# Pool makes the low parts of the projections' weights, the indexer sees 384 query tokens, and the branch for crowded experts goes behind the stores

## The chip, the cores and the metric

The kernel runs on one core of one Trainium2 chip (trn2). The metric is the device time of one execution in microseconds (us). The engines are TensorE (PE; PEld is its loading of weights), VectorE (DVE), ScalarE (ACT), GpSimd (POOL) and SyncE (SP); SP issues nearly all transfers between the chip's main memory and the on-chip memory, which 16 transfer engines carry out.

## What is computed

One decoder layer over 512 tokens of width 1024, then a final norm. In float32, shortened from the reference:

```
h = rms_norm(x, g_mix)
qa, ka, va, qb, kb, vb, qi, ki, wi, ga, gb = split(h @ w_in)     # 8 heads of 64 each; qi: 8 indexer heads; ki: one
qa, ka, qb, kb, qi, ki = rope(...)
o_a = block-sparse attention(qa, ka, va)                         # at 512 tokens: plain causal attention
score[t, s] = sum_h wi[t, h] * relu(qi[t, h] . ki[s])            # indexer, s <= t
o_b = attention(qb, kb, vb) over the 128 best keys s of each t by score
x = x + (sigmoid(ga) * (o_a @ w_proj_a) + sigmoid(gb) * (o_b @ w_proj_b)) @ w_out
h2 = rms_norm(x, g_ffn)
group = argmax of 4 group logits; two best of the 8 experts in that group, with gates
x = x + sum over the two experts e of gate * ((silu(h2 @ w1[e]) * (h2 @ w3[e])) @ w2[e])     # 32 experts
return rms_norm(x, g_final)
```

A query t < 128 has at most 128 admissible keys, so all of them are selected for it whatever the scores are.

## The kernel before

**Precision.** A product that has to be nearly float32 is made of three products of a one-pass format: a value is split into a high part (ACT copies it to that format) and a low part (the value minus the high part, a subtraction by DVE or Pool). `split` is this pair; `halves_of` loads a chunk of weights in two halves of 512 KB, splits the first with DVE's subtraction and the second with Pool's. A chunk is 1024 x 256 weights of one projection; `chunk(name)` loads one of the 20 that pass through it (two more come through `load_split` and `halves_of` at the start), at raised priority. Three buffers hold raw halves ("raw"), two pairs hold high and low parts ("wh", "wl").

**Front half.** PE's program is an order written out by hand (`in_order`); the other engines are ordered by a planner that places instructions by dependence and priority. `proj_T` makes one block of 128 columns of a chunk, transposed, for all 512 tokens: 8 steps over the contraction of three products each. `two_blocks` makes both blocks of a chunk, `rope_of` rotates one, `q_stack` and `k_stack` split the result for the attention (`k_stack` has four subtractions on Pool for each block). `attend` runs one quad of heads in 8 steps, and between scores, transposes and values it lets a share of other work run (`run(work, cost)`; a step of `proj_T` counts 0.64). That other work is `others`: the indexer's queries qi0, then qi1, qa1 and ka1 mixed with `idx_scores` (the indexer's scores for the token blocks 1 to 3; block 0 is not scored), values, queries and keys of branch b, gates and merging. `topk` on DVE finds 128 keys for each query.

**Experts.** 32 experts in 8 groups of 4, weights in 24 pieces of 1 MB for each group (8 for w1, 8 for w3, 4 + 4 for the two halves of w2). `fetch` requests the next piece into a free slot of 8 KB per partition, `spend` frees a slot and fetches again; SP's program is in order (`ordered`). Each expert has room for 32 tokens (CAP). Per group: `up` with w1, `silu_of`, `gated`, `up` with w3, `hidden`, gathering of the next group's tokens, `hidden_T`, `down` for each half of the width, `parts_of` (split of the result), `combine` (products that spread the results to the tokens, and DVE's addition to x).

If an expert has more than 32 tokens, `rest_of_tokens` does the rest in a loop. That branch stands before group 6 (lines 1018 to 1032): the order by hand is closed, every engine loads the largest count (`nc.values_load`) and compares it. With these inputs no expert has more than 32 tokens, so the loop is skipped. Ahead of the branch 8 pieces are requested from ACT's queue (`BRIDGE`), and a few slots are held back for it (`kept`).

**End.** For the last group the second half of w2 is mixed with combining the first half (`first_half`); then for each block of 128 tokens: combine the second half, sum of squares, power on Pool, scaling of the first half on ACT and of the second on DVE, and two stores (8 stores of 256 KB in all). This end is ordered by the planner.

Of the kernel before, what the change touches and what calls it, by code (L numbers as in the profile page):

```python
# [21 lines left out]
P = 128  # L22
# [18 lines left out]

REST = 6
BRIDGE = 8
# [96 lines left out]
def layer_kernel(ctx: ExitStack, tc: tile.TileContext, xT, x, w_ki, w_ch, w_ab, w_out, g_mix, g_ffnk, g_fin, w_r, b_r,  # L140
# [46 lines left out]
    def load_split(src, pair=None, place=None):  # L187
        hi, lo = pair or w_pair()
        for _ in halves_of(hi, lo, src, place):
            pass  # L190
# [121 lines left out]
    def q_stack(name, ps):  # L312

        qs = Q[name[1:]] = S.get([P, 4, T], F32R, name)
        for b in range(2):
            r = rope_of(ps[b])
# [289 lines left out]
    gfn, have, kept = [], {}, [0]  # L606

    def fetch(n, queue=sp):
        for _ in range(n):
            if not todo or len(S.idle) <= kept[0]:  # L610
# [8 lines left out]
            queue.dma_start(out=have[q, i], in_=w_e[q, i])  # L619
# [261 lines left out]
    def transposed(gsel):  # L881
# [4 lines left out]
        selT = t2([P, T], F32R, name="selT", tag="selT")  # L886
# [5 lines left out]
    def gated(sel, G):  # L892
# [4 lines left out]
        return transposed(gsel.rearrange("p t e s -> p t (e s)"))  # L897
# [21 lines left out]
    def parts_of(ys):  # L919

        out = []
        for h in range(2):
            y = t2([P, 2, 512], F32R, name="y", tag="y")
# [4 lines left out]
    def combine(selT, y, c, t):  # L928
# [6 lines left out]
        dve.tensor_tensor(o, ps, o, ALU.add)  # L935

# [79 lines left out]
    waiting = []  # L1016
    for q in range(NQ):
        if q == REST:
            for f in waiting:
                f()  # L1020
            waiting = []
            kept[0] = 0
            fetch(BRIDGE, act)
            bridge.close()
            in_order.close()
            ordered.close()
            rv = nc.values_load(cint[0:1, 0:1], min_val=0, max_val=T)
            with tc.If(rv > CAP):
                rest_of_tokens()
            ordered.enter_context(tc.manual_schedule(engines={mybir.EngineType.SP}))  # L1030
            in_order.enter_context(tc.manual_schedule(engines={mybir.EngineType.PE}))
            fetch(len(S.idle))
        if q == REST - 1:
            bridge = ExitStack()
            bridge.enter_context(tc.manual_schedule(engines={mybir.EngineType.Activation}))
# [9 lines left out]
        selT, gate = gated(sel, G[:, :, QE * q:QE * (q + 1)])  # L1045
        h3 = two(pt_, "tr", "h3")
        for k in range(NK):
            if q == REST - 1 and k == 2:

                kept[0] = len(S.idle) + BRIDGE + 6  # L1050
# [113 lines left out]
```

## Time and profile before

| | before |
|---|---|
| median of 3 runs | 937.04 us (935.4 to 939.02) |
| the profiled execution's own time | 939.58 us |
| its span, first to last instruction | 937.5 us |
| PE busy | 875.8 us, 93% |
| DVE busy | 426.5 us, 45% |
| ACT busy | 278.5 us, 30% |
| POOL busy | 178.6 us, 19% |
| granted TensorE clock, mean | 0.984 |

Busy is time in which an engine had an instruction under way; products on PE overlap, so a busy PE is not PE at its peak. Queue names end in q (SPq); a row of SPq is a request for a transfer or a wait of that queue, not the transfer. In rows of operations, "out<-in" gives the program's names, then partitions x elements and type; a bracket at the end gives the idle time before and what ended it.

### The profile page before, as it was taken

The page shows a single profiled execution, that of the slowest core. Times are in us where ns is not written, and L with a number is a line of the kernel's source. Part 1 is how long each engine was busy: PE and PEld are TensorE (multiplying, and loading weights), DVE is VectorE, ACT ScalarE, POOL GpSimd, SP SyncE. Part 2 cuts the span into 40 slices and gives each one's busy share as a digit, 9 for nine tenths or more (in the row PEclk, how much of TensorE's full clock was granted, in tenths as well). Part 3 has the DMA queues.
Part 4 walks back from the last instruction along what each step waited for, and adds up shares of the span by engine and source line. Part 5 has one row for each costly group of instructions (what it writes and reads, how often), then busy time and mean ns, then how long its engine had stood idle before and what let it go on. Part 6 is the DMA issues. An engine that isn't in the chain of part 4 may idle for free. (4 is left out here: it accounts for less than half of the span.)

```text
span 937.5 us, 15635 instructions
## 1 busy us (share of the span) xinstructions
PE 875.8 (93%) x6436; PEld 518.0 (55%) x6436; DVE 426.5 (45%) x981; ACT 278.5 (30%) x585; POOL 178.6 (19%) x115
## 2 busy tenths in 40 slices
PE   7999989989999999899999999999998989599885
PEld 5897769768777877689834343422423223133221
DVE  3747899998545554641722323231421302313114
ACT  4546654553443554533510100010100100001013
POOL 1494335243114820600300000000000000000003
PEclk9999999999999999899999999999999999799998
DMA  8422112112214221574589999999999999989995
GB/s 324 153 81 68 46 46 91 45 45 91 68 68 180 90 91 50 188 289 180 208 359 420 420 420 421 420 419 420 419 421 420 421 420 419 417 330 418 422 419 201
DMA packets 41261, 244.49 MB, mean 261 GB/s; under 512 B 4961, under 2 KB 5345, under 8 KB 16609
## 3 DMA queue, kind: packets, MB, share of 16 engines
q1 hardware_dynamic: 40032, 235.06, 63.4%
q10 hardware_dynamic: 1152, 8.39, 2.2%
q8 instruction: 51, 0.84, 0.4%
q14 instruction: 26, 0.20, 0.1%
HBM read 241.33 MB, written 2.10 MB: 260 GB/s over the span
## 5 line engine op out<-in xcount | busy, mean ns | idle before, releaser
L868 PE MATMUL h<-we,xs 128*32 128x512 f32 x2048 | 237.4, 600 | 25.9 <-DMA we<-in_w_e_dram 16.7
L868 PEld LDWEIGHTS h<-we,xs 128*32 128x32 f32 x2048 | 59.0, 110 | 179.3 <-issue 111.9
L875 PE MATMUL y<-we,hT 128*32 128x512 f32 x1024 | 116.1, 595 | 3.0 <-DMA we<-in_w_e_dram 3.0
L266 PE MATMUL mm<-xh,wh 128*128 128x512 f32 x272 | 110.2, 405 | 0.8 <-DVE bias L404 0.8
L268 PE MATMUL mm<-xh,wl 128*128 128x512 f32 x272 | 107.7, 396 | 0.0
L267 PE MATMUL mm<-xl,wh 128*128 128x512 f32 x272 | 107.7, 396 | 0.0
L173 POOL TENSOR_TENSOR wl<-raw,wh 128x1024 fp32r<-128x1024 f32 (+1 forms) x23 | 64.4, 2801 | 135.0 <-ACT wh L172 76.9
L1094 POOL TENSOR_TENSOR fo<-x,gfn 128x512 f32<-128x512 f32 x4 | 5.0, 1272 | 446.4 <-DVE x L935 446.4
L935 DVE TENSOR_TENSOR x<-cps,x 128x512 f32<-128x512 f32 x64 | 43.3, 688 | 82.0 <-PE cps L933 81.9
L875 PEld LDWEIGHTS y<-we,hT 128*32 128x32 f32 x1024 | 30.1, 109 | 74.5 <-issue 56.7
L909 DVE SCALAR_TENSOR_TENSOR silu<-silu,gate,h 128x512 f32<-128x512 f32 x16 | 12.0, 748 | 114.7 <-PE h L868 113.7
L268 PEld LDWEIGHTS mm<-xh,wl 128*128 128x128 f32 x272 | 51.2, 188 | 12.4
L266 PEld LDWEIGHTS mm<-xh,wh 128*128 128x128 f32 x272 | 51.4, 189 | 11.8 <-issue 1.2
L267 PEld LDWEIGHTS mm<-xl,wh 128*128 128x128 f32 x272 | 51.3, 189 | 9.6
L172 ACT CAST wh<-raw 128x1024 fp32r<-128x1024 f32 (+1 forms) x46 | 45.6, 1028 | 32.2 <-DMA raw<-in_w_ch_dram 13.2
L903 ACT ACTIVATE silu<-h 128x512 f32<-128x512 f32 x16 | 9.6, 598 | 146.7 <-PE h L868 119.2
L172 ACT CAST y<-y 128x512 fp32r<-128x512 f32 x32 | 18.7, 586 | 113.6 <-PE y L875 113.6
L916 ACT COPY hT<-htr 128x512 f32<-128x512 f32 x16 | 8.7, 588 | 147.3 <-PE htr L914 147.3
L173 DVE TENSOR_TENSOR y<-y,y 128x512 fp32r<-128x512 f32 x32 | 22.0, 688 | 54.3 <-ACT y L172 54.3
L448 ACT ACTIVATE ps<-e,st 128x128 f32<-128x128 f32 (+3 forms) x64 | 33.5, 524 | 43.7 <-DVE st L447 43.5
L173 DVE TENSOR_TENSOR wl<-raw,wh 128x1024 fp32r<-128x1024 f32 (+1 forms) x23 | 31.9, 1386 | 27.2 <-ACT wh L172 22.6
L687 PE MATMUL mm<-woh,mt 128*128 128x256 f32 x128 | 36.5, 285 | 1.2 <-DVE mt L655 1.2
(201 smaller groups left out, 1569.2 us busy)
## 6 DMA issues: line engine op xcount, KB each, us to landing
we<-in_w_e_dram SPq DMA_DIRECT2D x184, 1024.0 KB, 19.8
raw<-in_w_ch_dram SPq DMA_DIRECT2D x44, 512.0 KB, 4.1
we<-in_w_e_dram ACTq DMA_DIRECT2D x8, 1024.0 KB, 16.1
raw<-in_w_ab_dram SPq DMA_DIRECT2D x8, 512.0 KB, 3.9
wraw<-in_w_out_dram SPq DMA_DIRECT2D x8, 512.0 KB, 4.9
xraw<-in_xT_dram SPq DMA_DIRECT2D x8, 256.0 KB, 6.5
xtok<-in_x_dram SPq DMA_DIRECT2D x4, 512.0 KB, 9.1
x<-in_x_dram SPq DMA_DIRECT2D x4, 512.0 KB, 5.1
```

Of the source, the lines that this page charges most:

```text
L172: act.copy(hi, raw)
L173: eng.tensor_tensor(lo, raw, hi.bitcast(F32), ALU.subtract)
L266: pe.matmul(ps, a, xk(k, 0), start=k == 0, stop=False)
L267: pe.matmul(ps, a, xk(k, 1), start=False, stop=False)
L268: pe.matmul(ps, lo[:, k, col:col + P], xk(k, 0), start=False, stop=k == NK - 1)
L448: act.activation(ps[:, :n], e[:, :n], AF.Exp, bias=st[:, 0:1], scale=-1.0, accum_out=st[:, 1:2])
L687: pe.matmul(ps, mt[t][:, 1, k], hi[:, k], start=False, stop=k == NK - 1)
L868: pe.matmul(ps[h][CAP * e:CAP * (e + 1)], xs[:, k, h, CAP * e:CAP * (e + 1)], w[:, e * FF:(e + 1) * FF], start=k == 0, stop=k == NK - 1)
L875: pe.matmul(ys[h][CAP * e:CAP * (e + 1)], hT[h][:, k, CAP * e:CAP * (e + 1)], w[:, e * FF:(e + 1) * FF], start=k == 0, stop=k == 3)
L903: act.activation(out[h], h1[h], AF.Silu)
L909: dve.scalar_tensor_tensor(a[h], a[h], gate[:, h:h + 1], h3[h], ALU.mult, ALU.mult)
L935: dve.tensor_tensor(o, ps, o, ALU.add)
```

## The change

Four parts. (1) `chunk` passes `engs=(pool, pool)`, so both halves' low parts are made by Pool. (2) Chunks qi0 and qi1 are projected, rotated and split for the tokens from 128 on only. (3) The branch goes from before group 6 to behind the stores; the count is loaded before group 1; `REST`, `BRIDGE`, `kept` and the requests from ACT's queue go. Inside the branch the second halves are combined, the loop runs, and the end is made once more. (4) The end has a written order on ACT, DVE and Pool also: x's second halves are put into PSUM by a product with the identity (`with_x`) during the last group's w3, the last products add to it there, and each token block is scaled and stored whole (4 stores of 512 KB). The last group's `selT` and last low parts have slots of their own, and its two PSUM pairs for the results change places.

The diff, cut to its core:

```diff
-REST = 6
-BRIDGE = 8
...
-    def halves_of(hi, lo, src, place=None):
+    def halves_of(hi, lo, src, place=None, engs=(dve, pool)):
 
         n = hi.shape[2]
         for a in range(0, NK, 4):
             raw = wp.tile([P, 4, n], F32, tag="raw", name="raw", bufs=N_RAW) if place is None else place[:, a:a + 4]
             sp.dma_start(out=raw, in_=src[:, a:a + 4])
-            split(hi[:, a:a + 4], lo[:, a:a + 4], raw, pool if a else dve)
+            split(hi[:, a:a + 4], lo[:, a:a + 4], raw, engs[a // 4])
...
-    def proj_T(w, col, ps, ks=range(NK)):
+    def proj_T(w, col, ps, ks=range(NK), t0=0):
 
         hi, lo = w
         for k in ks:
-            a = hi[:, k, col:col + P]
-            pe.matmul(ps, a, xk(k, 0), start=k == 0, stop=False)
-            pe.matmul(ps, a, xk(k, 1), start=False, stop=False)
-            pe.matmul(ps, lo[:, k, col:col + P], xk(k, 0), start=False, stop=k == NK - 1)
-            yield 0.64
+            a, xhi, xlo, o = hi[:, k, col:col + P], xk(k, 0)[:, t0:], xk(k, 1)[:, t0:], ps[:, t0:]
+            pe.matmul(o, a, xhi, start=k == 0, stop=False)
+            pe.matmul(o, a, xlo, start=False, stop=False)
+            pe.matmul(o, lo[:, k, col:col + P], xhi, start=False, stop=k == NK - 1)
+            yield 0.64 * (T - t0) / T
...
-    def rope_of(ps, rows=P):
-
-        u, r = t2([rows, T], name="ru"), t2([rows, T], name="r")
-        dve.tensor_tensor(r, ps, sinr[:rows], ALU.mult)
-        dve.stream_shuffle(u, r, [i ^ 1 for i in range(32)])
-        dve.tensor_tensor(ps, ps, cosr[:rows], ALU.mult)
-        dve.tensor_tensor(r, ps, u, ALU.add)
+    def rope_of(ps, rows=P, t0=0):
+
+        u, r, ps = t2([rows, T], name="ru")[:, t0:], t2([rows, T], name="r"), ps[:, t0:]
+        rv = r[:, t0:]
+        dve.tensor_tensor(rv, ps, sinr[:rows, t0:], ALU.mult)
+        dve.stream_shuffle(u, rv, [i ^ 1 for i in range(32)])
+        dve.tensor_tensor(ps, ps, cosr[:rows, t0:], ALU.mult)
+        dve.tensor_tensor(rv, ps, u, ALU.add)
         return r

     def chunk(name):
         with tc.high_priority(PRIO):
-            return load_split(w_ch[CHUNKS.index(name)])
+            return load_split(w_ch[CHUNKS.index(name)], engs=(pool, pool))
+
+    def first_token(name):
+
+        return P if name[:2] == "qi" else 0
 
     def two_blocks(name):
         w, ps = chunk(name), []
         for b in range(2):
             ps.append(bank())
-            yield from proj_T(w, b * P, ps[b])
+            yield from proj_T(w, b * P, ps[b], t0=first_token(name))
...
+            t0 = first_token(name)
+            r = rope_of(ps[b], t0=t0)
             for j, h, l in ((2 * b, LOW, UPP), (2 * b + 1, UPP, LOW)):
-                act.copy(qs[h, j], r[h])
-                pool.tensor_tensor(qs[l, j], r[h], qs[h, j].bitcast(F32), ALU.subtract)
+                act.copy(qs[h, j, t0:], r[h, t0:])
+                pool.tensor_tensor(qs[l, j, t0:], r[h, t0:], qs[h, j, t0:].bitcast(F32), ALU.subtract)
...
+    def with_x(ps, t):
+
+        pe.matmul(ps, ident, x2t(t)[:, 512:], start=True, stop=False, skip_group_check=True)
+        return ps
...
-        if q == REST:
-            for f in waiting:
-                f()
-            waiting = []
-            kept[0] = 0
-            fetch(BRIDGE, act)
-            bridge.close()
-            in_order.close()
-            ordered.close()
-            rv = nc.values_load(cint[0:1, 0:1], min_val=0, max_val=T)
-            with tc.If(rv > CAP):
-                rest_of_tokens()
-            ordered.enter_context(tc.manual_schedule(engines={mybir.EngineType.SP}))
-            in_order.enter_context(tc.manual_schedule(engines={mybir.EngineType.PE}))
-            fetch(len(S.idle))
-        if q == REST - 1:
-            bridge = ExitStack()
-            bridge.enter_context(tc.manual_schedule(engines={mybir.EngineType.Activation}))
+        if q == 1:
+            over = nc.values_load(cint[0:1, 0:1], min_val=0, max_val=T)
...
+            if q == last and k % 2:
+                t, (p, tag) = k // 2, ((pa, "sc"), (pa, "sc"), (pm, "mm"), (pb, "o"))[k // 2]
+                total[t] = with_x(p.tile([P, 512], F32, tag=tag, name="fin"), t)
...
+    for e in (mybir.EngineType.Activation, mybir.EngineType.DVE, mybir.EngineType.Pool):
+        in_order.enter_context(tc.manual_schedule(engines={e}))
+    fo = [S.get([P, D], F32, "fo") for _ in range(NT)]
+    junk, ylast = S.get([P, NT, 512], F32, "junk"), S.get([P, 2, 2, 512], F32R, "ylast")
+    FIRST, SECOND = slice(0, 512), slice(512, D)
+
+    def square(t, c, v):
+        act.activation(junk[:, t], v, AF.Square, scale=D ** -0.5, accum_out=ssp[:, t, c:c + 1])
+
+    def first_half(t):
+        square(t, 0, x2t(t)[:, FIRST])
+        pool.tensor_tensor(fo[t][:, FIRST], x2t(t)[:, FIRST], gfn[0][:, FIRST], ALU.mult)
+
+    def second_half(v):
+        for t in range(NT):
+            square(t, 1, v[t])
+            dve.tensor_tensor(fo[t][:, SECOND], v[t], gfn[0][:, SECOND], ALU.mult)
+        for t in range(NT):
+            r = ssp[:, t, 2:3]
+            pool.tensor_tensor(r, ssp[:, t, 1:2], ssp[:, t, 0:1], ALU.add)
+            pool.tensor_tensor(r, r, half[:, 0:1], ALU.pow)
+            if t == 1:
+                act.activation(fo[t], fo[t], AF.Copy, scale=r)
+            else:
+                dve.tensor_scalar(fo[t], fo[t], r, None, ALU.mult)
+        for t in (0, 2, 1, 3):
+            sp.dma_start(out=out[t * P:(t + 1) * P], in_=fo[t])
+
+    def eps():
+        dve.tensor_scalar(ssp[:, :, 0:1], ssp[:, :, 0:1], EPS, None, ALU.add)
+
+    y = parts_of(ys)
+    ys = two(pt_, "tr", "y1")
+    for t in range(NT):
+        combine(selT, y, 0, t)
+        first_half(t)
+        if t % 2:
+            use(q, 2 * NK + 4 + t // 2, down, t // 2, ys, hT)
+    for k in range(2, 4):
+        use(q, 2 * NK + 4 + k, down, k, ys, hT)
+    eps()
+    y = parts_of(ys, ylast)
+    for t in range(NT):
+        sl = selT[:, t * P:(t + 1) * P]
+        for part in range(2):
+            pe.matmul(total[t], sl, y[t // 2][:, part], start=False, stop=part == 1, skip_group_check=True)
+    second_half(total)
     in_order.close()
     ordered.close()
...
+    with tc.If(over > CAP):
+        for t in range(NT):
+            combine(selT, y, 1, t)
+        rest_of_tokens()
+        for t in range(NT):
+            first_half(t)
+        eps()
+        second_half([x2t(t)[:, SECOND] for t in range(NT)])
```

## Rows read from the trace of the kernel before

**Rows 1.** Page, parts 2 and 6: slices; requests, KB, us to landing.

```profile
GB/s 324 153 81 68 46 46 91 45 45 91 68 68 180 90 91 50 188 289 180 208 359 420 420 420 421 420 419 420 419 421 420 421 420 419 417 330 418 422 419 201
...
we<-in_w_e_dram SPq DMA_DIRECT2D x184, 1024.0 KB, 19.8
```

**Rows 2.** Windows: us, PE, PEld, DVE, ACT, POOL busy, PEclk, DMA share, GB/s.

```profile
60.00:210.00 150.00, 139.97 (x865) 115.02 (x864) 131.09 (x344) 82.33 (x179) 66.64 (x41) 0.99 0.19 60
210.00:370.00 160.00, 160.00 (x837) 126.91 (x836) 92.58 (x218) 72.23 (x152) 50.00 (x25) 1.00 0.27 89
...
500.00:600.00 100.00, 100.00 (x890) 34.28 (x891) 26.94 (x44) 8.71 (x16) 0.00 (x0) 1.00 1.01 420
...
820.00:840.00 20.00, 20.00 (x188) 6.00 (x184) 1.29 (x2) 1.20 (x2) 0.00 (x0) 1.00 0.76 310
```

**Rows 3.** Instructions of the branch, line 1028: ns, first and last start us.

```profile
L1028 SPq EVENT_SEMAPHORE  x8: 17/17/17, 826.6 to 827.2; - x8
...
L1028 SPq COMPARE_BRANCH  x1: 50/50/50, 787.3 to 787.3; - x1
L1028 PEldq COMPARE_BRANCH  x1: 6426/6426/6426, 802.9 to 802.9; - x1
```

**Rows 4.** The register load of the count, line 1027: ns, start us.

```profile
L1027 PEldq TENSOR_LOAD <-cint x1: 489/489/489, 802.3 to 802.3; - x1
```

**Rows 5.** Timeline of PE: start us, us, operation.

```profile
62.49 0.39 PE L268 MATMUL mm<-xh,wl 128*128 128x512 f32 x1
...
72.06 0.39 PE L267 MATMUL mm<-xl,wh 128*128 128x512 f32 x1
...
85.33 0.34 PE L443 MATMUL ps<-hika,qa 128*128 128x384 f32 x1
85.50 0.34 PE L444 MATMUL ps<-loka,qa 128*128 128x384 f32 x1
```

**Rows 6.** Page, part 5: low parts of weights on both engines.

```profile
L173 POOL TENSOR_TENSOR wl<-raw,wh 128x1024 fp32r<-128x1024 f32 (+1 forms) x23 | 64.4, 2801 | 135.0 <-ACT wh L172 76.9
...
L173 DVE TENSOR_TENSOR wl<-raw,wh 128x1024 fp32r<-128x1024 f32 (+1 forms) x23 | 31.9, 1386 | 27.2 <-ACT wh L172 22.6
```

**Rows 7.** Waits of PE between 60 and 210 us: total, times, longest.

```profile
PE ps L443 <- DVE e L450: 5.4, 4, 2.1
PE ips L400 <- DVE bias L404: 3.0, 5, 1.3
```

**Rows 8.** Timelines of DVE and PE around 155 us.

```profile
152.38 3.00 DVE L173 TENSOR_TENSOR wl<-raw,wh 128x1024 fp32r<-128x1024 f32 x1
...
156.89 0.35 PE L443 MATMUL ps<-hika,qa 128*128 128x256 f32 x1 [1.81 <-DVE e L450]
```

**Rows 9.** Timeline of POOL between 50 and 65 us.

```profile
50.46 11.63 POOL L330 TENSOR_TENSOR loka<-r,hika 64x512 fp32r<-64x512 f32 x8
62.17 2.41 POOL L173 TENSOR_TENSOR wl<-raw,wh 128x1024 fp32r<-128x1024 f32 x1
```

**Rows 10.** POOL's timeline near 30 us, and DVE's line 366 (ns, min/median/max).

```profile
29.91 2.43 POOL L173 TENSOR_TENSOR wl<-raw,wh 128x1024 fp32r<-128x1024 f32 x1 [0.72 <-ACT wh L172]
...
L366 DVE TENSOR_SCALAR dg<-cb,rstd x4: 276/278/2419, 30.0 to 32.7; 128x128 f32<-128x128 f32 x4
```

**Rows 11.** Timeline of the end: last products, first and last store.

```profile
922.03 1.92 PE L875 MATMUL y<-we,hT 128*32 128x512 f32 x16 [0.54 <-DMA we<-in_w_e_dram]
...
929.01 0.35 SPq L1108 DMA_DIRECT2D out_dram<-fo  x1
...
934.07 0.41 SPq L1110 DMA_DIRECT2D out_dram<-fo  x1
```

**Rows 12.** Transfers by line, stores; window of their transfer.

```profile
out_dram<-fo SPq DMA_DIRECT2D x8, 256.0 KB, 2.2
...
935.00:936.00 1.00, 0.00 (x0) 0.00 (x0) 0.00 (x0) 0.00 (x0) 0.00 (x0) 0.50 1.01 383
```

**Rows 13.** DVE's line 415 by form, 512 columns.

```profile
L415 DVE TENSOR_SCALAR bias<-bias 128x512 f32<-128x512 f32 x1 | 0.4, 420 | 0.0
```

More of the change, by code (lines that the diff above doesn't have):

```diff
@@ L185, in w_pair, with load_split @@
         return [wp.tile([P, NK, n], F32R, tag=name, name=name, bufs=2) for name in ("wh", "wl")]
-    def load_split(src, pair=None, place=None):
+    def load_split(src, pair=None, place=None, engs=(dve, pool)):
         hi, lo = pair or w_pair()
-        for _ in halves_of(hi, lo, src, place):
+        for _ in halves_of(hi, lo, src, place, engs):
             pass
@@ L605, in layer_kernel, with fetch @@
     todo = [(q, i) for q in range(NQ) for i in range(PIECES)]
-    gfn, have, kept = [], {}, [0]
-    def fetch(n, queue=sp):
+    gfn, have = [], {}
+    def fetch(n):
         for _ in range(n):
-            if not todo or len(S.idle) <= kept[0]:
+            if not todo or not S.idle:
                 return
@@ L618, in fetch @@
             have[q, i] = S.get([P, QE * FF], F32, "we")
-            queue.dma_start(out=have[q, i], in_=w_e[q, i])
+            sp.dma_start(out=have[q, i], in_=w_e[q, i])
     def spend(q, i):
@@ L879, in two, with transposed @@
         return [pool_.tile([P, 512], F32, tag=tag, name=name) for _ in range(2)]
-    def transposed(gsel):
+    def transposed(gsel, place):
         tr = bank("gtr")
@@ L885, in transposed @@
             pe.transpose(tr[:, t * P:(t + 1) * P], gsel[:, t], ident)
-        selT = t2([P, T], F32R, name="selT", tag="selT")
+        selT = t2([P, T], F32R, name="selT", tag="selT") if place is None else place
         gate = small([P, 2], "gate")
@@ L890, in transposed, with gated @@
         return selT, gate
-    def gated(sel, G):
+    def gated(sel, G, place=None):
         gsel = t2([P, NT, QE, CAP], name="gsel", tag="hT")
@@ L1044, in layer_kernel @@
         a = silu_of(h1)
-        selT, gate = gated(sel, G[:, :, QE * q:QE * (q + 1)])
+        selT, gate = gated(sel, G[:, :, QE * q:QE * (q + 1)],
+                           S.get([P, T], F32R, "selT") if q == last else None)
         h3 = two(pt_, "tr", "h3")
         for k in range(NK):
-            if q == REST - 1 and k == 2:
-                kept[0] = len(S.idle) + BRIDGE + 6
             use(q, NK + k, up, 1, k, range(2), h3, xs)
+            if q == last and k % 2:
+                t, (p, tag) = k // 2, ((pa, "sc"), (pa, "sc"), (pm, "mm"), (pb, "o"))[k // 2]
+                total[t] = with_x(p.tile([P, 512], F32, tag=tag, name="fin"), t)
         hidden(a, h3, gate)
@@ L1064, in layer_kernel @@
                 gather(xs, sel, 1, b)
-        ys = two(pa, "sc", "y0")
+        ys = two(pt_, "tr", "y0") if q == last else two(pa, "sc", "y0")
         for k in range(4):
             use(q, 2 * NK + k, down, k, ys, hT)
-        y = parts_of(ys)
         if q == last:
             break
+        y = parts_of(ys)
         ys = two(pt_, "tr", "y1")
@@ L1080, in layer_kernel @@
+    second_half(total)
     in_order.close()
     ordered.close()
-    fo = [S.get([P, D], F32, "fo") for _ in range(NT)]
-    def squares(t, c):
-        junk = t2([P, 512], name="junk", tag="hT")
-        act.activation(junk, x2t(t)[:, c * 512:(c + 1) * 512], AF.Square, scale=D ** -0.5, accum_out=ssp[:, t, c:c + 1])
-    def first_half(t):
-        combine(selT, y, 0, t)
-        squares(t, 0)
-        dve.tensor_scalar(ssp[:, t, 0:1], ssp[:, t, 0:1], EPS, None, ALU.add)
-        pool.tensor_tensor(fo[t][:, :512], x2t(t)[:, :512], gfn[0][:, :512], ALU.mult)
@@ L1096, in layer_kernel @@
-    ys = two(pt_, "tr", "y1")
-    for k in range(4):
-        use(q, 2 * NK + 4 + k, down, k, ys, hT)
-        first_half(k)
-    y = parts_of(ys)
-    for t in range(NT):
-        combine(selT, y, 1, t)
-        squares(t, 1)
-        r = small([P, 1], "fin")
-        pool.tensor_tensor(r, ssp[:, t, 1:2], ssp[:, t, 0:1], ALU.add)
-        pool.tensor_tensor(r, r, half[:, 0:1], ALU.pow)
-        act.activation(fo[t][:, :512], fo[t][:, :512], AF.Copy, scale=r)
-        sp.dma_start(out=out[t * P:(t + 1) * P, :512], in_=fo[t][:, :512])
-        dve.scalar_tensor_tensor(fo[t][:, 512:], x2t(t)[:, 512:], r, gfn[0][:, 512:], ALU.mult, ALU.mult)
-        sp.dma_start(out=out[t * P:(t + 1) * P, 512:], in_=fo[t][:, 512:])
+    with tc.If(over > CAP):
[6 more added lines that the diff above has]
+        second_half([x2t(t)[:, SECOND] for t in range(NT)])
```

10 lines of the change are left out of this document (5 added, 5 removed).

## The prediction

> **What bounds the kernel now.** I read the page's transfer rates first, because they divide the run: up to about 405 us the transfer engines have little to do, from then on they run near one ceiling [rows 1]. Then the windows, for each stage [rows 2]: between 60 and 370 us PE is busy nearly throughout while transfers take 0.19 to 0.27 of their time, so this front half goes at PE's pace. From 500 us on transfers stand at 420 GB/s and a share of 1.01, so the experts go at the pace of their weights. PE waits for weights right up to the last piece (0.54 us before the last 16 products) [rows 11]. So three things count: when PE begins on the experts' weights (an earlier front half moves everything behind it by as much), bytes lost while the stream should be full, and what lies behind the last piece.
>
> One stretch of the stream is not full: from 820 to 840 us it moved 310 GB/s. The missing 110 of 420 over 20 us are 5.2 us of transfer [rows 2]. The branch's own instructions say why [rows 3]: SP reaches the branch at 787.3 us and issues nothing until eight semaphore waits end between 826.6 and 827.2 us. The eight pieces that ACT requested ahead of the branch are 20 us of traffic at 420 GB/s, so the engine that refills the queue sits there until the queue is empty.
>
> **The change part by part.** *Branch moved behind the stores.* The wait of SP in the middle goes, with the eight requests on ACT's queue and the slots held back for them; those eight go back into SP's order. SP has requests in flight for 19.8 us [rows 1], so the register load now put ahead of group 1 (0.49 us on PE, like the others [rows 4]) is covered on SP by that backlog and on PE by its waits for weights; uncovered it would be 0.5 us. Gain 5.2 us, because the stream is what sets the end from there on: between 0 (should PE or the slots take over) and 5.2. I take 5.2.
>
> *Indexer's queries for 384 tokens.* Two chunks of two blocks, each 24 products: 96 products of 512 columns become 384 wide. PE starts 512-wide products 0.233 us apart (41 steps from 62.49 to 72.06) and 384-wide ones 0.17 us (85.33 to 85.50; 0.175 by columns), though each still loads its weights [rows 5]. 96 x 0.058 = 5.6 us. The rotation on DVE and the copies shrink too. PE is the pace at qi0; during qi1 it shares the pace with DVE, so the lower bound is half, 2.8 us. I take 5.6.
>
> *Low parts by Pool.* Twenty chunks pass through here; for each, the first half's subtraction moves from DVE to Pool. The page has 23 halves on each, 1.39 us in the mean on DVE and 2.80 us on Pool [rows 6]. DVE gives up 20 x 1.39 = 28 us. Where this matters is 60 to 210 us, with DVE busy 131 of 150 us [rows 2]. There PE was released late by DVE for 5.4 us in the attention's scores and 3.0 us in the indexer's, 8.4 us together [rows 7]. The longest kind is legible: at 152.38 us a low part holds DVE for 3.00 us, and the scores behind it reach PE at 156.89 us after an idle 1.81 us [rows 8]. Not every one of these waits has a low part in front: rotation and top-k stand there too. Bounds 0 and 8.4; I take half, 4.2 us.
>
> The same move has a price. Pool has room on average (67 of 150 us busy, then 50 of 160 [rows 2]; twenty more halves add some 56 us over the front half), but it works in order and its queue is locally full. At 50.46 us it begins eight subtractions for the first keys, 11.63 us, and then takes the second half of qi0 at 62.17 us [rows 9]. The first half, until now DVE's, would now come behind the same eight: ready at 62.17 + 2.41 = 64.58, where PE wants it with its third product at 62.49 [rows 5]. That is 2.1 us late; the second half lands at 67.0, some 0.3 us later than 12 more products need. PE's order is fixed, so both are lost: 2.4 us, between 0 (if the planner puts qi0 ahead of the keys) and 2.4.
>
> A second place is the first chunk of values. Its Pool half runs from 29.91 us, and DVE's four scalings of the identity just then took 0.28 us each but once 2.42 us [rows 10]: one waited for Pool to finish. With two halves in a row on Pool this can happen twice, 2.4 us more for DVE, which PE in its fixed order would feel at most whole. 0 to 2.4 us; I take 1.0. For the other eighteen chunks the two halves in a row are ready up to 2.4 us later; a chunk's 48 products last 48 x 0.233 = 11 us, and no row shows PE waiting for Pool, so most is covered. Bounds 0 and 18 x 0.3 = 5.4 (0.3 being what the second half of qi0 misses by); nearest to 0, I take 1.0. Together the price is 4.4 us.
>
> Here a rule of the Trainium skill speaks against the change. "GPSIMD Engine Reference", section "Engine selection", puts elementwise work on VectorE, because Pool takes about twice as long for two inputs; the trace agrees (2.80 against 1.39 us [rows 6]). If the difference showed at every chunk, 20 x 1.41 = 28 us would be lost; by the rows only what is late for PE is lost, 4.4 us. The rows decide the sum, and the rule stands beside the rival on the slow side.
>
> *The end.* Now the last products begin at 922.03 us and stores are issued from 929.01 to 934.07 us [rows 11]; one lands 2.2 us after its issue [rows 12], so at 936.3, and the span ends 1.2 us later. In the new order the sums of squares and the output's first halves stand in front of the last low parts on ACT, DVE and Pool, and would hold them up if they were late; they need the sums of the half before, and run while the last three pieces come in (3 MB, 7.5 us at 420 GB/s). From the last product on the chain is as long as before: cast, low part, product, square, power, scaling. Scaling is over 1,024 columns: DVE took 0.42 us for 512 of such a form [rows 13], so at most 0.84 each, three on DVE. I put the first store at 929 as now, the fourth at about 931.6. Four stores of 512 KB need 5.5 us at 383 GB/s, however they are issued; a store of 256 KB has 0.7 us of transfer in its 2.2 us, so 1.5 besides [rows 12]. 929 + 1.5 + 5.5 = 936.0: 0.3 us earlier. The branch adds eight waits on SP as in the middle (0.6 us [rows 3]), which run beside the stores' landing. I take 0.3 us, between -2.3 (rival 4) and +0.8 (a first store 0.5 us earlier).
>
> The four products that put x into PSUM are full-width float32: by the last row of weights (eight quarter-width products in 1.92 us [rows 11]) about 0.9 us each, 3.6 us over eight pieces in each of which PE waits about 0.5 us. Covered; without cover 3.6 us in the last group, partly caught up before the end.
>
> **Sum.** 5.2 + 5.6 + 4.2 - 4.4 + 0.3 = 10.9 us. The profiled execution took 939.58 us with a span of 937.5; it would come to 928.7. It lies 2.5 us over the median of 937.04, to which I apply the same difference: 926.1 us. Half a per cent (4.7 us, down to 932.4 or up to 941.7) is about what a measurement of this kernel tells from no change.
>
> **Rivals.**
> 1. *The front half gains nothing.* Late low parts and DVE's waits eat the shorter queries. Left is the branch and the end: 937.0 - 5.5 = 931.5 us. For it: Pool's queue at 50 to 62 us; against it: PE's 8.4 us of waits are real and a low part lies ahead of the longest kind.
> 2. *DVE's relief is complete* and qi0's low parts pass the keys: 5.2 + 5.6 + 8.4 + 0.8 = 20.0, or 917.0 us. Against it: DVE keeps top-k and rotations there.
> 3. *The hole in the stream stays*, because slots, not SP, run short there: 926.1 + 5.2 = 931.3 us. For it: the stream fell short once more, to 180 and 208 GB/s in two slices before 470 us, after it had filled the slots [rows 1]; against it: it stays at 417 to 421 in all slices from there to the hole, with the same slots.
> 4. *The branch costs at the end.* PE's jump took 6.4 us in the middle, under full traffic [rows 3]. If SP's does so after its last store, 931.6 + 6.4 + 0.6 of waits + 1.2 of closing = 939.8, the end comes 2.3 us later than now: 937.04 - 10.6 + 2.3 = 928.7 us. "Runtime: NRT & Kernel Launch", section "Instruction fetch mechanics", in the Trainium skill says that a taken branch to a place outside the fetched window must wait for a fetch by DMA; PE's 6.4 us agree with it.
> 5. *Pool becomes the pace of the projections* (the slow side). Place: chunks while Pool also makes low parts of keys and queries. To be slower by 0.5% it has to lose the 15.3 us of the other terms (5.2 + 5.6 + 4.2 + 0.3) and 4.7 more, 20 us or 1.0 us at every chunk; at 1.41 us each (28 us) the time is 937.0 - 15.3 + 28 = 949.7 us. Against it: Pool is idle more than half of each stretch, and it decides only where every chunk's half comes late.
>
> **How the numbers follow.** Forecast 0.45 (922 to 930), rival 1 0.20, rival 2 0.12, rival 3 0.06, rival 4 0.10, rival 5 0.07. Faster: forecast, rivals 2 and 4, 0.12 of rival 1 and 0.04 of rival 3: 0.83. Same: 0.08 + 0.02 = 0.10. Slower: rival 5, 0.07. The range leaves out rival 5, the faster half of rival 2 and the slowest quarter of rival 1: 917 to 932.5 us.
>
> **What would show it.** No window under 415 GB/s between 500 us and the last piece; 384-wide products 0.175 us apart; PE waiting for "wl" from Pool near 62 us (right if 2 us, rival 2 if none); PE's waits for DVE between 60 and 210 us down by half; the experts' first products some 5.4 us earlier (5.6 + 4.2 - 4.4); the last store issued about 9.6 us behind the start of the last piece's products (12.0 now). The prediction is wrong if PE waits for Pool at many chunks, if the stream has a new hole, or if instructions behind the stores last longer than the stores.

## The result and the profile after

The changed kernel takes 932.52 us (median of 7 runs, 931.78 to 933.08), the kernel before 937.04 in the same comparison: 4.5 us faster by the medians. Over all runs the ratio is 0.9944 [0.9931, 0.9958]; the quotient of the two medians (0.9952) lies within that interval. The forecast was 926.1 us with a range of 917 to 932.5. The profiled execution took 931.78 us with a span of 929.9.

The stretches that answer to [rows 2], and two of the stream's end (windows of the kernel after; columns as there):

```profile
60.00:210.00 150.00, 139.86 (x872) 117.37 (x870) 123.61 (x355) 84.52 (x184) 85.84 (x54) 0.99 0.21 68
210.00:370.00 160.00, 160.00 (x862) 127.20 (x860) 73.86 (x190) 70.11 (x148) 58.86 (x31) 1.00 0.27 87
820.00:840.00 20.00, 17.17 (x184) 7.46 (x184) 4.26 (x6) 1.07 (x2) 0.00 (x0) 1.00 1.01 420
904.00:908.00 4.00, 3.48 (x22) 1.43 (x22) 2.16 (x4) 1.74 (x5) 2.20 (x2) 1.00 0.82 340
908.00:912.00 4.00, 4.00 (x36) 1.06 (x34) 2.52 (x3) 1.34 (x4) 2.85 (x3) 1.00 0.43 178
```

DVE is relieved (123.6 us busy for 131 between 60 and 210 us, 73.9 afterwards) and the hole at 820 to 840 us is filled. But the stream now ends ragged: for some six us half of the transfer share is unused. Before ran full to 920 us and stopped; this window of it is the next one:

```profile
920.00:924.00 4.00, 3.41 (x32) 0.68 (x24) 0.03 (x1) 0.79 (x3) 0.00 (x0) 1.00 0.11 45
```

PE's waits between 60 and 210 us in the kernel after, against [rows 7]:

```profile
PE mm L265 <- POOL wl L170: 4.0, 1, 4.0
PE ps L446 <- DVE e L453: 1.7, 2, 1.3
PE ips L403 <- POOL qi L322: 1.4, 1, 1.4
...
PE ips L403 <- DVE bias L407: 0.5, 2, 0.3
```

Here ps and e belong to the attention's scores, ips and bias to the indexer's, and wl is a low part of weights. The 8.4 us of waits for DVE (e and bias) fell to 2.2, and a new one of 4.0 us for Pool stands where the prediction put 2.4. With the smaller rows, the waits of PE listed for this window add up to 10.0 us before and to 10.0 us after. POOL and PE there, in the timelines after, against [rows 9]:

```profile
51.42 10.69 POOL L333 TENSOR_TENSOR loka<-r,hika 64x512 fp32r<-64x512 f32 x8
62.18 2.59 POOL L387 TENSOR_TENSOR kst<-r,kst 64x512 fp32r<-64x512 f32 x2
64.85 7.02 POOL L170 TENSOR_TENSOR wl<-raw,wh 128x1024 fp32r<-128x1024 f32 x3
```

```profile
62.94 0.34 PE L264 MATMUL mm<-xl,wh 128*128 128x384 f32 x1
67.25 0.44 PE L265 MATMUL mm<-xh,wl 128*128 128x384 f32 x1 [3.97 <-POOL wl L170]
```

Not only the eight subtractions for the first keys (loka) but also the two for the indexer's keys (kst) went ahead of qi0's low part.

The end after, against [rows 11] (timelines of PE and SP):

```profile
912.97 1.92 PE L878 MATMUL y<-we,hT 128*32 128x512 f32 x16 [0.54 <-DMA we<-in_w_e_dram]
914.83 2.53 PE L1119 MATMUL fin<-ylast,selT 128*128 128x512 f32 x8
```

```profile
919.96 3.85 SPq L1100 DMA_DIRECT2D out_dram<-fo  x4
```

The last piece's products begin 9.1 us earlier than in before, the first store is issued 7.0 us behind them as in before and the last one 10.5 us behind them (12.0 in before), but the span ends only 7.6 us earlier. And 7.6 us of span are 4.5 us of median, because before's profiled execution lay 2.5 us over its median and after's 0.7 under it.

### The profile page after: what moved, and what is told of

It is laid out like the page before. It is cut to its first block, busy times and chain, and to the rows that moved or that the text cites. A ratio compares the mean times of both kernels' runs of the same rounds, so it can differ in the third digit from the quotient of the medians.

```text
span 929.9 us, 15650 instructions
## 1 busy us (share of the span) xinstructions
PE 873.2 (94%) x6444; PEld 516.0 (55%) x6444; DVE 398.8 (43%) x957; ACT 275.4 (30%) x582; POOL 209.2 (23%) x135
## 4 chain that ended last, share of the span: by engine, by line
PE 57%; DMA 29%; DVE 6%; POOL 3%; ACT 2%; issue 2%; SPq 0%; POOLq 0%; ACTq 0%; DVEq 0%
DMA we<-in_w_e_dram 28%; PE h L871 9%; PE y L878 7%; PE mm L263 5%; PE mm L265 5%; PE mm L264 5%; PE ops L474 2%; PE mm L690 2%; PE mm L688 2%; PE mm L689 2%; PE cps L935 1%; PE mm L517 1%; PE mm L519 1%; PE tr L462 1%; PE mm L518 1%
## 5 line engine op out<-in xcount | busy, mean ns | idle before, releaser
L170 POOL TENSOR_TENSOR wl<-raw,wh 128x1024 fp32r<-128x1024 f32 (+1 forms) x43 | 101.7, 2388 | 110.5 <-ACT wh L169 55.1
L265 PE MATMUL mm<-xh,wl 128*128 128x512 f32 (+1 forms) x272 | 106.9, 393 | 4.0 <-POOL wl L170 4.0
L263 PE MATMUL mm<-xh,wh 128*128 128x512 f32 (+1 forms) x272 | 109.7, 403 | 0.5 <-DVE bias L407 0.5
L264 PE MATMUL mm<-xl,wh 128*128 128x512 f32 (+1 forms) x272 | 106.2, 390 | 0.0
L938 DVE TENSOR_TENSOR x<-cps,x 128x512 f32<-128x512 f32 x60 | 41.1, 689 | 92.7 <-PE cps L936 92.6
L265 PEld LDWEIGHTS mm<-xh,wl 128*128 128x128 f32 x272 | 51.6, 190 | 15.4 <-POOL wl L170 4.3
L169 ACT CAST wh<-raw 128x1024 fp32r<-128x1024 f32 (+1 forms) x46 | 45.6, 1027 | 41.5 <-DMA raw<-in_w_ch_dram 19.1
L689 PE MATMUL mm<-wol,mt 128*128 128x256 f32 x128 | 37.1, 290 | 0.0
```

The lines of the kernel that those rows point to most:

```text
L169: act.copy(hi, raw)
L170: eng.tensor_tensor(lo, raw, hi.bitcast(F32), ALU.subtract)
L263: pe.matmul(o, a, xhi, start=k == 0, stop=False)
L264: pe.matmul(o, a, xlo, start=False, stop=False)
L265: pe.matmul(o, lo[:, k, col:col + P], xhi, start=False, stop=k == NK - 1)
L689: pe.matmul(ps, a, lo[:, k], start=False, stop=False)
```

## The experiments

For each run the profile gives three lengths: when the experts' first product begins (the front half), from there to the start of the last product of the last piece (the stream), and from there to the span's end (the end). Beside them stands how long TensorE was granted 1.2 GHz rather than 2.4 ahead of 470 us; each such microsecond costs half of one where PE sets the pace. All in us:

| kernel | median | front | at 1.2 GHz | stream | end |
|---|---|---|---|---|---|
| before | 937.04 | 465.7 | 10.2 | 457.7 | 14.2 |
| b_again | 938.49 | 464.3 | 10.2 | 457.7 | 14.2 |
| e_qi | 939.50 | 466.9 | 13.7 | 457.9 | 14.2 |
| e_pool | 936.97 | 463.4 | 10.2 | 458.0 | 14.2 |
| p_one | 935.94 | 462.7 | 10.2 | 457.9 | 14.2 |
| h_nobranch | 933.93 | 463.3 | 3.4 | 455.0 | 14.6 |
| e_end | 933.12 | 459.7 | 3.4 | 454.5 | 15.4 |
| e_end2 | 933.63 | 461.9 | 6.8 | 454.7 | 15.9 |
| after | 932.52 | 459.8 | 3.4 | 454.5 | 15.6 |
| a_nobranch | 930.27 | 460.6 | 3.4 | 454.3 | 13.2 |
| f_qi0 | 928.86 | 456.5 | 3.4 | 454.6 | 15.3 |
| g_full | 928.72 | 457.0 | 3.4 | 454.6 | 15.3 |
| b1 | 929.20 | 455.4 | 3.4 | 454.6 | 15.5 |
| s_split | 934.13 | 461.2 | 6.8 | 456.0 | 15.4 |
| s_split2 | 932.74 | 459.5 | 6.8 | 456.0 | 15.4 |

Before, timed beside these, had medians of 937.3 to 938.5. The intervals of the single ratios are 1.2 to 1.9 us wide to either side, so a difference between two of these kernels is known to some 2 us; the profiled lengths are of one execution each.

**b_again**, before without any edit.

> The kernel before, unchanged, profiled once more. Theory A says that the profiled execution that the forecast was summed against was a long one, and that the excess lies in one place: a second one has a span nearer 935, with the experts' first product near 465.7 us again and the missing microseconds somewhere behind it. Rival: the two profiles are alike within 0.5 us at each marker (first experts' product, last piece's products, span's end), and the 2.5 us over the median are scatter outside the span.

Its span was 936.2 us. Stream and end agree with the first profile to 0.1 us; the whole difference of 1.4 us lies in the front. So theory A was wrong about the place, and the table can be read: stream and end repeat, the front scatters.

**e_qi, e_pool**: one edit of the front each, put into before.

```diff
-            pe.matmul(ps, a, xk(k, 0), start=k == 0, stop=False)
...
+            a, xhi, xlo, o = hi[:, k, col:col + P], xk(k, 0)[:, t0:], xk(k, 1)[:, t0:], ps[:, t0:]
+            pe.matmul(o, a, xhi, start=k == 0, stop=False)
...
-            return load_split(w_ch[CHUNKS.index(name)])
+            return load_split(w_ch[CHUNKS.index(name)], engs=(pool, pool))
```

> Before with the indexer's queries for 384 tokens alone. If the term of the forecast (5.6 us) is right, the time is 931.4 us (937.0 - 5.6), the experts' first product near 460. If PE is not the pace where the shorter products stand, it is 934.2 (half, the lower bound) or up to 937. A rival on the whole-run side: an earlier front moves the full stream but the end follows by less, so that the first experts' product gains more than the end does.

> Before with the low parts of the projections' weights on Pool alone, queries for all tokens. By the forecast's terms (4.2 - 4.4) nothing: 937.2 us, with PE waiting for Pool's low part near 62 us for 2 to 4 us and its waits for DVE between 60 and 210 us down by half. If DVE's relief is worth more than Pool's lateness it is 933 to 936; if Pool paces the projections (rival 5), over 942.

The shorter queries alone gain nothing: ratio 1.0017 [1.0001, 1.0032]. PE reaches the indexer's first scores at 73.0 us, 4.4 us earlier than in b_again (77.4). Then (e_qi, timelines of DVE, POOL and PE):

```profile
86.00 3.43 DVE L173 TENSOR_TENSOR wl<-raw,wh 128x1024 fp32r<-128x1024 f32 x1
```

```profile
85.97 2.38 POOL L173 TENSOR_TENSOR wl<-raw,wh 128x1024 fp32r<-128x1024 f32 x1 [4.39 <-PE ps L450]
```

```profile
90.91 0.80 PE L406 MATMUL ips<-kst,qi 128*128 128x512 f32 x1 [3.27 <-DVE r L297]
```

A low part on DVE begins 0.03 us behind one on Pool and takes 3.43 us rather than 1.22; the last step of a rotation behind it is late, PE waits 3.3 us, and 6.8 us at 1.2 GHz begin within this wait. Pool alone gives 0.9989 [0.9974, 1.0004]: PE waits 4.2 us for Pool at 62 us, at the place forecast for the changed kernel, its waits for DVE's e and bias fall from 8.0 us (b_again) to 2.6, and by the time the two nearly cancel. PE's waits in e_pool:

```profile
PE mm L268 <- POOL wl L173: 4.2, 1, 4.2
...
PE ps L443 <- DVE e L450: 1.4, 1, 1.4
...
PE ips L400 <- DVE bias L404: 1.2, 3, 0.7
```

**e_end, e_end2**: the changed kernel without its front edits (`engs` and `first_token` as in before), two profiles.

> The changed kernel without its two edits of the front half: only the branch behind the stores and the new end. Forecast: 937.0 - 5.2 - 0.3 = 931.5 us. Theory A: what the hole cost was only the time in which the slowest transfer engines stood still, about 3 us, the rest comes back as a run-out at the end in which half of the engines have nothing left (DMA share near 0.5 for some 6 us), and the new end costs 1.5 us: 937.0 - 3.2 + 1.5 = 935.3 us. Rival B: the hole's 5.2 us are gained whole and only the end loses (1.5): 933.3 us, with no such run-out.

> The branch and the end alone once more, for a second profile. Its instructions up to 470 us are those of before, engine by engine, yet its first experts' product came 4.6 us earlier than in the second profile of before. Theory A: that is chance (stretches in which TensorE was granted half its clock, 3.4 us in place of 10.2): this profile has the first product anywhere between 460 and 466 us, in step with its half-clock stretches. Rival: it is the program: the first product is at 459.7 us again, whatever the clock.

0.9949 [0.9929, 0.9969] and 0.9954 [0.9940, 0.9968]: the branch and the end alone make nearly the whole gain of the change. The time is that of rival B (933.3), but the run-out that it excludes is there (shares of 0.65, 0.51 and 0.31 between 906 and 912 us in e_end), and the stream is 3.2 and 2.9 us shorter, not 5.2; with an end 1.2 and 1.7 us longer theory A explains 2.0 us or less. Against before in their own comparisons the two gained 4.9 and 3.7 us. The other 2.5 to 2.9 us lie in the front, in which no instruction differs from before. The half-clock stretches moved, but one thing was the same both times. DVE and POOL in e_end2, against [rows 8]:

```profile
151.72 1.22 DVE L170 TENSOR_TENSOR wl<-raw,wh 128x1024 fp32r<-128x1024 f32 x1
```

```profile
151.82 3.37 POOL L170 TENSOR_TENSOR wl<-raw,wh 128x1024 fp32r<-128x1024 f32 x1 [0.94 <-ACT wh L169]
```

Here DVE is first by 0.1 us, takes 1.22 us, and Pool is the one that is held. In before, b_again and h_nobranch Pool is first by 0.5 us, DVE takes 3.0 us, and PE waits 1.8 us.

**p_one**: before, with that one chunk's low parts both on Pool.

```diff
+            return load_split(w_ch[CHUNKS.index(name)], engs=(pool, pool) if name == "qb0" else (dve, pool))
```

> Before with the low parts of one chunk alone, the first of the second attention's queries, both on Pool. In all profiles with the branch in the middle or left out, DVE's half of this chunk begins 0.5 us behind Pool's and takes 3.0 us, and the scores reach PE 1.8 us late; in both profiles of branch and end alone, with the same instructions in the same order, it begins ahead of Pool's and takes 1.22 us, with no such wait. Theory A: this accident, and the half-clock stretch that follows PE's wait, is what is left of the gain of the branch and the end alone (4.5 us, of which the stream and the end explain 2): without it before takes 934.5 to 936 us, with no wait for e near 156 us. Rival: PE makes it up until 210 us; 937.5 us.

0.9972 [0.9958, 0.9985], 2.5 us faster, within theory A's bounds; the wait for e at 156 us is gone, and PE's waits between 60 and 210 us add up to 7.7 us for 10.0. A stretch of 3.4 us at 1.2 GHz is still there (at 185 us), so the gain is not that stretch. With 3.2 from the stream and 1.2 lost at the end this makes 4.5, between the gains of e_end and e_end2. Why the two programs differ by 0.4 us in ACT's cast at that place was not found.

**h_nobranch, a_nobranch**: before and after without the branch (tokens beyond 32 per expert are left out; there are none). Cut from h_nobranch; a_nobranch loses its own load and branch:

```diff
...
-            rv = nc.values_load(cint[0:1, 0:1], min_val=0, max_val=T)
-            with tc.If(rv > CAP):
-                rest_of_tokens()
...
```

> Before without its branch (the experts' tokens beyond 32 are left out, of which this data has none), with its old end and its old front. It prices the hole in the stream alone. Theory A (the hole is worth only the 3 us in which the slowest transfer engines stood still, the rest comes back as a run-out at the end): 937.5 - 3.2 = 934.3 us, DMA share near 0.5 for about 6 us behind the full stream. Rival B (the forecast's term, 5.2 us): 932.3 us. Rival C (the gain of the changed end, not of the hole): 937 us, the stream ends no earlier.

> The changed kernel without its branch at the end (tokens beyond 32 left out, of which there are none) and so without the register loads. It prices what the branch costs behind the stores. If the register loads among the last scalings and the 2.3 us of the third store's issue come from the branch: last products to span's end 15.4 us rather than 16.9, 931.0 us. If they don't (the end's 1.5 us are the four stores of 512 KB themselves): 932.5 us as the changed kernel. If the branch is the end's bound (rival 4): 928 us.

The hole is worth 0.9962 [0.9949, 0.9975], 3.4 us by median and 2.7 of stream: theory A, with its run-out (windows of h_nobranch):

```profile
908.00:912.00 4.00, 3.90 (x24) 1.49 (x23) 3.47 (x6) 0.53 (x1) 2.02 (x2) 1.00 0.76 317
912.00:916.00 4.00, 3.72 (x40) 0.93 (x32) 0.00 (x0) 0.00 (x0) 2.97 (x3) 1.00 0.38 160
```

At the end the branch costs 932.52 - 930.27 = 2.25 us by medians of two comparisons (1.7 by the ratios 0.9944 and 0.9926, 2.4 by the profiled ends); without it the new end is 1.0 us shorter than the old one. Where the 2.25 us are shows in the transfers between 918 and 930 us, first in after:

```profile
q1 hardware_dynamic: 576, 2.10, 44.3%
q14 instruction: 5, 0.04, 1.1%
q8 instruction: 1, 0.02, 0.8%
```

and its windows there, which have a dent at 923 and a tail (last two columns: share, GB/s):

```profile
922.00:923.00 1.00, 0.00 (x0) 0.00 (x0) 0.00 (x0) 0.00 (x0) 0.00 (x0) 0.50 0.98 385
923.00:924.00 1.00, 0.00 (x0) 0.00 (x0) 0.00 (x0) 0.00 (x0) 0.00 (x0) 0.50 0.63 242
927.00:928.00 1.00, 0.00 (x0) 0.00 (x0) 0.00 (x0) 0.00 (x0) 0.00 (x0) 0.50 0.06 25
```

a_nobranch has no instruction transfers there and no dent:

```profile
q1 hardware_dynamic: 576, 2.10, 43.9%
...
923.00:924.00 1.00, 0.00 (x0) 0.00 (x0) 0.00 (x0) 0.00 (x0) 0.00 (x0) 0.50 1.00 393
```

The trace has each store's landing in 16 parts. In after 15 parts of the first store land between 922.4 and 922.6 us and one at 924.4; in a_nobranch all between 923.0 and 923.2. In after an instruction transfer of 8 KB (0.52 us, at 920.05) and one of 16 KB (1.47 us, at 920.92) took 2.0 us together, about what the late part is late. That they are the cause is argued and not shown: on which transfer engine they ran the trace does not say. The last landing is 1.3 us late for the late parts at the end, and from there to the span's end it is 1.8 us with the branch, 1.0 without. The dent at 923 us has another origin: SP's issue of the third store took 2.28 us in after, 2.2 in e_end2 and 2.0 in f_qi0, which all show a dent, and 0.80 in e_end, which has the branch and no dent. It is not what sets the end: from the first store's issue to the last landing it is 7.9 us in e_end, 8.2 in after and 6.5 in a_nobranch. SP's own jump, which rival 4 had priced at 6.4 us, took 0.05 us.

**s_split, s_split2**: after, with the experts' up-projections in products of 256 columns (for h = 0, for both halves), for 6 pieces of 8.

```diff
+                for c in (0, 256) if h == 0 and 0 < k < NK - 1 else (None,):
```

> The changed kernel with the experts' up-projections for the first four experts' half (h = 0) in two products of 256 columns, for six of eight pieces: the same arithmetic in some 25% more TensorE instructions in the stream. Theory A: the lag of half of the transfer engines comes from TensorE's instruction fetches (16 KB, 1.07 us each), which take turns on these engines: fetches come closer, the lag grows faster (jumps every 95 us rather than 121) and ends near 7.5 us rather than 6.5, and the end comes about 1 us later: 933.5 us. Rival: the lag has nothing to do with the instructions (it goes by bytes or by time): jumps every 121 us, 6.5 us at the end, 932.5 us.

> The same with both halves' products split, some 50% more TensorE instructions in the stream. Theory A: jumps every 80 us, lag near 9 us at the end, 2 to 3 us later than the changed kernel: 935 us. Rival: 6.5 us of lag and 932.5 us. If TensorE itself becomes the pace (its wait for each piece, 0.56 us now, goes to nothing), the run tells nothing of the lag.

They ask why the stream ends ragged. By the trace's landings in after, a piece's 16 parts land 2.0 us apart at 500 us, and 6.5 us at the end; the gap jumps by 1.5 us every 120 us. Before shows 1.9 growing to 5.1 at the hole, and 1.7 behind it: in the hole the late half catches up. What recurs is TensorE's instruction transfers, 16 KB and 1.07 us each; their count in the whole run is in the page's queue part, in the order after, s_split, s_split2:

```profile
q8 instruction: 52, 0.85, 0.4%
```

```profile
q8 instruction: 58, 0.95, 0.4%
```

```profile
q8 instruction: 64, 1.05, 0.5%
```

The 1,536 and 3,072 instructions more on TensorE (products and weight loads, by the pages' counts) make 6 and 12 transfers more, one for 256 instructions. Between 480 and 930 us the transfers are 30, 36 and 41, so 20% and 37% more rather than the 25% and 50% expected; the jumps come every 120, 101 and 85 us in the mean, with each eighth transfer in all three runs, and the gap ends at 6.5, 7.9 and 8.0 us. Bytes are the same and run time nearly so, and the rival falls: the lag goes with TensorE's instructions. Why a jump comes with each eighth transfer was not looked into. The stream is 1.5 us longer in both (456.0); by median they are 1.6 and 0.2 us slower than after (934.13 and 932.74), by the ratios 1.0 and 0.1. Theory A's 2 to 3 us for the second did not come: it has as many jumps in the stream as the first, four.

**f_qi0, g_full, b1**: after with qi0's low parts on DVE; the same with queries for 512 tokens; f_qi0 with the first values' chunk split as in before.

```diff
+            return load_split(w_ch[CHUNKS.index(name)], engs=(dve, dve) if name == "qi0" else (pool, pool))
...
-        return P if name[:2] == "qi" else 0
+        return 0
...
+            return load_split(w_ch[CHUNKS.index(name)], engs={"qi0": (dve, dve), "va0": (dve, pool)}.get(name, (pool, pool)))
```

> The changed kernel with the low parts of the first chunk of indexer's queries on DVE alone, the other chunks on Pool. PE's wait of 4.0 us for Pool at 63 us goes. Theory A: DVE paces 75 to 210 us, so the wait is mostly absorbed by 210 us in the changed kernel, and removing it moves the experts' first product by 1 us or less: 932 us. Rival: the front is PE's, the 4 us come off at the end too: 928.5 us.

> The changed kernel with the first queries' low parts on DVE alone, and the indexer's queries for all 512 tokens again. Beside the kernel that differs from it only in the queries (928.9 us) it prices the shorter queries where Pool is no longer late; beside the one with branch and end alone (933.1 and 933.6) it prices DVE's relief without Pool's lateness at 63 us. Theory A: PE is the pace at the first chunk of queries only, in the second DVE is; the shorter queries are worth about half of the 5.6 us: 931.7 us. Rival: worth nothing, as in the run with the shorter queries alone: 929 us. Rival: worth the 5.6 us whole: 934.5 us.

> The changed kernel with the first queries' low parts on DVE alone and the first values' chunk split between DVE and Pool as before; a candidate for the best version. PE's wait of 0.8 us behind the scaled identity (32 us) goes. If that wait is on the path, 928.1 us; if PE catches up or DVE's low part at the chunk is late in its turn, 928.9 us or up to 930.

f_qi0 takes 928.86 us, 0.9906 [0.9891, 0.9920] of before and 3.7 us under after: the late low part of qi0 costs that much, and DVE does not absorb it (the rival). g_full takes 928.72, 0.9906 [0.9890, 0.9922]: the shorter queries are worth nothing here too, within some 2 us. PE's waits between 60 and 210 us, f_qi0 first, then g_full:

```profile
PE ips L403 <- DVE r L294: 3.2, 2, 2.6
PE ps L446 <- DVE e L453: 1.7, 2, 1.4
PE ops L474 <- ACT pt L464: 1.3, 3, 0.6
PE ips L403 <- DVE bias L407: 0.6, 2, 0.3
PE mm L263 <- DVE bias L407: 0.5, 1, 0.5
```

```profile
PE ips L403 <- DVE bias L407: 1.4, 4, 0.7
PE ps L446 <- DVE e L453: 1.4, 1, 1.4
PE mm L263 <- DVE bias L407: 0.8, 1, 0.8
PE ops L474 <- ACT pt L464: 0.5, 1, 0.5
PE ips L403 <- POOL qi L322: 0.5, 1, 0.5
```

7.3 against 4.6 us: PE comes to the indexer's scores earlier and waits for the rotated queries (r). The two programs differ in PE's order also: `run` counts a step of a shorter projection 0.48 rather than 0.64, so the shares of `attend` end elsewhere. Between the first and the second group of attention scores g_full has one pair of the indexer's scores, f_qi0 three; the attention's later scores come 3 to 6 us later in f_qi0 up to 290 us, the projections up to 5 us earlier. No run has the shorter products in the old order.

b1 (929.20) cannot be told from f_qi0: the wait of 0.8 us for the scaled identity is gone from its profile and its front is 1.1 us shorter, but its median is 0.3 us longer. f_qi0, g_full and b1 are the fastest versions, ahead of both kernels of the study.

## Why the prediction was wrong

By medians the forecast's terms came out like this (gains positive):

| term | forecast | measured | from |
|---|---|---|---|
| hole in the stream | 5.2 | 3.2 | e_end's stream; h_nobranch 2.7 to 3.4 |
| queries for 384 tokens | 5.6 | 0 | g_full, f_qi0; e_qi -1.6 |
| DVE's relief | 4.2 | 4.4 to 4.9, and 2.5 | e_end and e_end2 to g_full; p_one, whose gain e_end and e_end2 already have |
| Pool late | -4.4 | -3.7 | f_qi0 to after (qi0 alone) |
| end | 0.3 | -1.2 | e_end; new end +1.0, branch -2.25 |

The measured terms add up to 5.2 to 5.7 where 4.5 was measured; the rest is within what medians of 4 to 12 runs can tell. How well terms add is itself known to some 2 us only: e_pool, with DVE's relief and Pool's lateness in one run, gained 1.0 us where these rows make 3.2 to 3.7.

**The step that failed most** is "I take 5.6" for the queries. The products did get shorter (0.176 us apart), but the step took PE for the pace of qi0 and half of qi1, and set its lower bound at 2.8. What was measured is 0, within some 2 us. That PE is busy is not yet that PE is the pace: [rows 2] showed DVE at 131 of 150 us in the same window, and [rows 7] PE's waits for it. PE's time saved comes back as waits for the rotation and the scores. From qi0's first product to the first scores of the last quad of heads (312.9 us in g_full, 312.5 in f_qi0) the products that are 512 or 384 wide take 4.2 us less in f_qi0 and the waits 2.9 us more; 0.6 us more went because qi0 began that much later, 0.3 on the rest, and 0.4 us is left. Why the saving is 4.2 us rather than 5.6 (the other products came 1.4 to 1.6 us longer in sum), and what share of the waits the changed order has, is open. The bound should have been 0. This is rival 1 in its effect: on top of the branch and the end, the two front edits gave 0.6 to 1.1 us, for 5.4 forecast.

**Luck.** The experts' first product was forecast 5.4 us earlier, and by the first two profiles it came 5.9 us earlier (465.7 to 459.8). But e_end, with the front of before, has it at 459.7 and e_end2 at 461.9: the front edits account for some 2 us of it at most. In the same way the branch and the end came near their forecast of 5.5 us (4.9 and 3.7) with 2.0 us or less from the terms that it named; the rest lay in the front, where p_one points to the accident near 152 us. And Pool's -4.4 is near the measured -3.7 only in sum: 2.4 was for qi0, which cost 3.7, and of the two terms of 1.0 us the one for the first values shows as a wait of 0.8 us, without which b1 is no faster, the other nowhere: PE waits for Pool's low parts of weights at no other place up to 470 us.

**The hole** was mis-sized. The step took the missing GB/s of the whole window. But the average runs over 16 engines of which half had run dry early, because they were ahead by 5.1 us. What sets the end is the late half, and it stood still for some 3 us: its last landing before the hole is at 826.6 us and its next at 832.4, 5.8 us for a step that is 2.5 in the full stream. The lead of the others is no gain: with the hole gone it comes back as a ragged end, the window 908 to 912 at 0.43.

**The end.** Without the branch the new end gained more than forecast (1.0 us for 0.3). The branch was priced at nothing, "beside the stores' landing"; it cost 2.25 us, and its instruction transfers, which stand in front of the stores' late parts, are the likely reason. Rival 4 had the place, with SP's jump for the mechanism and a size that didn't occur.

**Right**: PE's wait for Pool near 62 us and its cause (size 4.0 for 2.4, as kst also went ahead), the waits for DVE down by more than half, no window under 415 GB/s up to the run-out, the first store at 7 us (the last one is issued 10.5 us behind the last piece's start, for 9.6). The four products with x took 1.1 us each for 0.9 and are covered: the stream is 454.3 us in a_nobranch and 455.0 in h_nobranch, which has none. One reading was off without effect on the sum: the transfers do not run near their ceiling from 405 us on, but fall again (44 GB/s between 430 and 435 us, 3 between 445 and 450) and are full from 480 us. The Trainium skill's rule in "GPSIMD Engine Reference", section "Engine selection", did not decide: no run shows Pool's longer subtraction at every chunk, only at qi0. DVE's relief was sized too low by the table, since half of the waits was taken; most of them went (8.4 to 2.2 us).

## What to carry to other kernels

Shorten the work of an engine only where the window says that no other engine is nearly as busy; else bound the gain at zero and test it alone, on top of the other edits. Price a hole in a stream by how long the slowest transfer engine stands still, not by the missing average. And a front of 460 us in which engines race for a port moves by some 2 us for 0.4 us of shift: compare lengths that repeat (stream, end) rather than one span.

## What was not expected of the hardware

Low parts on DVE and Pool at once: whichever is first runs on, and the other pays. DVE 1.22 us alone, 3.00 and 3.43 behind Pool; Pool 2.40 alone, 3.37 behind DVE. In e_qi Pool's ends at 88.35 us and DVE's 1.1 us after it. The Trainium skill says in "SBUF — State Buffer", section "SBUF: two separate sides", that only the port pair shared by these two engines causes contention on the engines' side, and that it is an exclusive lock; the runs agree.

With TensorE's instruction transfers of 16 KB (1.07 us each) half of the transfer engines fell behind, by 1.5 us for every eight, to 6.5 us at the stream's end (after). "Runtime: NRT & Kernel Launch", section "Instruction fetch mechanics", in the Trainium skill names blocks of 16 KiB (256 instructions) and calls their cost mostly hidden; the block agrees with s_split and s_split2 (6 and 12 transfers for 1,536 and 3,072 instructions). TensorE itself was not seen to wait for them here, but the slowest engines of a full stream lost 1.5 us to every eight.

The same wait of PE for DVE of 2.8 to 3.1 us (for mt, the merged output of the two attentions), near 382 us, was followed by 6.8 us at 1.2 GHz in before, b_again and e_end2, by 3.4 in e_end and f_qi0, and by none in after and h_nobranch. This and the low parts both move the front by some us; that they are all of its scatter, and of that of before's time, is not shown.
